# One step of a hybrid SSD and attention encoder: order of transposes, banks, evictions and operands at the edges of its stages

## The chip, the core and the metric

The kernel runs on one core of a Trainium2 chip. A core has TensorE (PE in the profile; PEld is its weight load), VectorE (DVE), ScalarE (ACT), GpSimd (POOL), SyncE (SP, which issues most DMAs here), an on-chip memory (SBUF) and eight accumulator banks (PSUM) of 512 float32 columns each. The metric is the device time of the whole program in microseconds, the median of several runs.

## The reference

One inference step over 1024 prompt tokens and 32 sample tokens with 1024 features, two layers, all float32:

```python
for i in range(DEPTH):                       # DEPTH = 2
    hn = rmsnorm(h, ln_w[i])
    if i == 0: y = ssd_mixer(hn, ...)        # in-projection, causal conv, chunked scan, gate, norm, out-projection
    else:      y = mla_mixer(hn, ...)        # low-rank q / kv, norms, rotary keys, block-causal attention, out-projection
    h = h + y
    g = sigmoid(rmsnorm(h, ple_norm_w[i]) @ ple_gate_w[i])
    h = h + (p[i] @ ple_up_w[i]) * g
```

Prompt and sample go through the same weights; the sample also has a convolution cache, a state and 1024 cached keys. The SSD mixer's projection gives, beside x, B, C and z, one step size dt for each of 32 heads: `dt = softplus(dt + bias)`, `Acs = cumsum(dt * A)` in chunks, and the scan weighs its rows with dt and with exponentials of differences of Acs.

## The kernel before

Activations lie with features on the 128 partitions and tokens on the free axis. A float32 product is made of three reduced ones: weights and operands are split into a high part (wh, hh, yh) and a rest (wl, hl, yl), and `gemm` (L239) issues, for every block k of 128 features, wh times high, wh times rest and wl times high into one bank. `load_weight` (L192) loads a block of 8 x 128 x 128 (SP), rounds it (ACT, L204) and takes the rest (POOL, L205); two or three such blocks have buffers at a time.

Nobody wrote down the order in which an engine's queue holds its work. A planner goes through the program with its own estimate of each instruction's duration and gives every engine a fixed order; buffers go to whoever's turn it is in that order, and an instruction waits for its operands and for the readers of the buffer that it takes over. So an edit at one place can move the order behind it.

**SSD phase** (`phase_ssd`, L301). The 1060 token columns (1024 prompt, a gap, 32 sample) go in three tiles of 384, 384 and 292. `normalise` (L318) makes the three tiles' normed operands hh and hl, 8 feature blocks each. `mblock` (L341) multiplies weight blocks with the tiles: a tile's result takes one of three mm banks and is evicted by `evac`. The heads are the first three blocks, dt (32 columns, `gemm_stacked`), B and C of group 0; L416 calls them tile by tile. Then follow, as `conv_block` (L487), blocks x(0,0) and x(0,1). Between them VectorE works out dt's 32 rows: `stk` holds dt, Acs and a third row set, and nine transposes (L482) bring it to `tokT`, tokens on the partitions. `stk` and its helpers lie in a pool that is closed after L483; the pool `work` (L485), with the scan's buffers ex, eb and y, is opened on the same space. For each of eight groups g the loop at L639 issues `scan_group(g)` (small products and exponentials in five chunks), the next group's B and C, the gate z of the group before, the next group's two x blocks, and `finish` of the group before. A block's raw result takes one of 6 `raw` buffers, a convolved one one of 6 `cx` buffers, and x, B and C hold theirs until their scan is done. In the last group `up_product` (L267) multiplies the layer's embeddings with their up weights in 8 blocks of three pieces of 352 columns, evicted by ACT (L290), and stores them.

**From there on** the columns are 1056 in two halves of 528 (HB), a half's product being two banks of 264 columns (`mm2`, three pairs). `gemm2` (L675) makes such a product: first all feature blocks for the left 264 columns, then all for the right. It is used by `phase_out` (L706; out-projections of both layers, with 16 and 8 feature blocks, output blocks m = 0..7, for each half), by `phase_ple` (L759; the gates) and by `phase_mla_in` (L797). `phase_out` loads a half's operands (yraw, five buffers), splits them on ACT and DVE into 33 buffers (yhl) that take both halves' rows in turn, and loads a weight block of 8 feature blocks wherever `part` (L727) comes to one. In the first half of the first out-projection three output blocks go ahead with the first 8 rows, while the others still come.

Then follow the MLA projections, the sample's attention, the prompt's attention, the second out-projection and the second gate; the change leaves the text of the attention parts as it was.

## Time and profile before

| | us |
|---|---|
| median of 3 runs (2000.93 to 2001.71) | 2001.32 |
| the profiled execution, its own time | 2003.33 |
| its span, first to last instruction | 2001.6 |
| PE busy (x12763) | 1927.1 |
| DVE busy | 1215.0 |
| ACT busy | 1069.0 |
| POOL busy | 999.9 |

In rows of the profile, `mm<-hh,wh` is a product that writes tile mm and reads hh and wh; L245 is its line in kernel.py, often a helper's. `128x292` are partitions and columns, x9 the number of instructions merged into one row. A row of the timeline has start, length, engine, line, operation, tiles; in brackets the idle time before it and what ended that. Products overlap their successors in PE's pipeline, so the step from start to start is what one costs, not its listed length. PEclk is the share of TensorE's clock that was granted.

### The profile page before, as it was taken

To read this page: it belongs to the slowest core of one execution; us is meant where nothing else is said; L and a number is where in the kernel's file an instruction comes from. 1 tells how busy PE (TensorE), PEld (TensorE's weight loads), DVE (VectorE), ACT (ScalarE), POOL (GpSimd) and SP (SyncE) were. 2 spreads that over 40 slices of the span, in tenths; PEclk is the share of its full clock that TensorE was granted. 3 is DMA by queue.
4 is the path that set the end of the run, shared out by engine and by line. 5 is a ranking of instruction groups with operands and counts; after the bars stand their busy time and mean duration, and the time that the engine had idled before them with its cause. 6 is when DMAs were issued, how large, how long until landed. Compare 5 with 4: busy or idle time off the path is not lost. (4 is left out here: it accounts for less than half of the span.)

```text
span 2001.6 us, 32532 instructions
## 1 busy us (share of the span) xinstructions
PE 1927.1 (96%) x12763; PEld 1773.0 (89%) x12763; DVE 1215.0 (61%) x1525; ACT 1069.0 (53%) x1998; POOL 999.9 (50%) x828
## 2 busy tenths in 40 slices
PE   7999999999999999999998999998899999999999
PEld 6989899999999998999998899777677877779999
DVE  7888674846657574452367543454667677755544
ACT  4345555454555558343244331777587878864331
POOL 5652424343443445554678452223556666645762
PEclk9999999999999999999999999999799999999999
DMA  4134433424233346553333221424412221416442
GB/s 141 43 83 104 93 86 83 106 74 103 75 94 91 78 118 233 173 174 123 101 120 121 83 75 65 152 85 124 102 47 57 61 72 41 119 57 196 125 129 72
DMA packets 110731, 204.26 MB, mean 102 GB/s; under 512 B 18225, under 2 KB 60721, under 8 KB 110449
## 3 DMA queue, kind: packets, MB, share of 16 engines
q1 hardware_dynamic: 105328, 193.04, 32.9%
q0 software_dynamic: 2944, 7.04, 1.8%
q8 instruction: 100, 1.64, 0.3%
q10 hardware_dynamic: 2304, 2.10, 0.3%
q14 instruction: 55, 0.44, 0.1%
HBM read 156.81 MB, written 38.83 MB: 98 GB/s over the span
## 5 line engine op out<-in xcount | busy, mean ns | idle before, releaser
L205 POOL TENSOR_TENSOR wl<-wraw,wh 128x1024 fp32r<-128x1024 f32 (+3 forms) x183 | 374.6, 2048 | 394.3 <-ACT wh L204 365.2
L245 PE MATMUL mm<-hh,wl 128*128 128x384 f32 (+1 forms) x1136 | 372.5, 328 | 0.0
L245 PE MATMUL mm<-hh,wh 128*128 128x384 f32 (+1 forms) x1136 | 372.3, 328 | 0.0
L245 PE MATMUL mm<-hl,wh 128*128 128x384 f32 (+1 forms) x1136 | 370.5, 326 | 0.0
L245 PE MATMUL pso<-yhl,wh 128*128 128x264 f32 x1536 | 283.8, 286 | 3.6 <-DVE yhl L259 2.2
L204 ACT ACTIVATE wh<-wraw 128x1024 fp32r<-128x1024 f32 (+3 forms) x181 | 157.2, 869 | 242.1 <-PE pso L245 103.7
L245 PEld LDWEIGHTS pso<-yhl,wh 128*128 128x128 f32 x1536 | 239.8, 189 | 5.3 <-DVE yhl L259 3.4
L245 PE MATMUL pso<-yhl,wl 128*128 128x264 f32 x768 | 219.2, 286 | 3.9 <-POOL wl L205 3.9
L245 PEld LDWEIGHTS mm<-hh,wh 128*128 128x128 f32 x1136 | 214.9, 189 | 3.5 <-issue 3.1
L245 PEld LDWEIGHTS mm<-hl,wh 128*128 128x128 f32 x1136 | 214.8, 189 | 1.2 <-issue 0.5
L245 PEld LDWEIGHTS mm<-hh,wl 128*128 128x128 f32 x1136 | 214.6, 189 | 0.8 <-issue 0.2
L496 DVE SCALAR_TENSOR_TENSOR cx<-raw,pv,cx 128x1060 f32<-128x1060 f32 x96 | 142.5, 1489 | 45.9 <-ACT cx L494 45.2
L559 ACT ACTIVATE ex<-ex,tokT 128x128 f32<-128x128 f32 (+1 forms) x288 | 87.0, 380 | 133.9 <-DMA ex<-acs_d 131.8
L245 PE MATMUL psi<-yhl,wh 128*128 128x264 f32 x832 | 153.6, 285 | 2.5 <-ACT yhl L258 1.7
L1346 PE MATMUL st<-qk 128*128 128x512 f32 (+2 forms) x576 | 150.3, 372 | 4.9 <-ACT pf L1352 4.1
L245 PEld LDWEIGHTS pso<-yhl,wl 128*128 128x128 f32 x768 | 145.2, 189 | 4.6 <-POOL wl L205 4.5
L245 PE MATMUL pg<-hH,wl 128*128 128x264 f32 x512 | 145.9, 285 | 2.5 <-POOL wl L205 2.5
L245 PE MATMUL pg<-hH,wh 128*128 128x264 f32 x512 | 145.9, 285 | 0.0
L245 PE MATMUL pg<-hL,wh 128*128 128x264 f32 x512 | 145.7, 285 | 0.0
L572 POOL TENSOR_TENSOR hm<-hT,cd_all 128x256 f32<-128x256 f32 x64 | 54.2, 848 | 160.4 <-DVE hT L574 95.4
L1328 DVE TENSOR_REDUCE mx<-s 128x1 f32<-128x128 f32 (+2 forms) x192 | 102.2, 550 | 52.0 <-PE s L1326 50.4
L245 PEld LDWEIGHTS psi<-yhl,wh 128*128 128x128 f32 x832 | 129.4, 188 | 3.9 <-ACT yhl L258 2.1
(546 smaller groups left out, 4649.5 us busy)
## 6 DMA issues: line engine op xcount, KB each, us to landing
wraw<-in_inW SPq DMA_DIRECT2D x48, 512.0 KB, 3.5
ex<-acs_d SPq DMA_DIRECT2D x32, 512.0 KB, 5.5
wraw<-in_outW SPq DMA_DIRECT2D x32, 512.0 KB, 3.7
yraw<-y_d SPq DMA_DIRECT2D x32, 264.0 KB, 4.6
u<-u_d SPq DMA_DIRECT2D x32, 264.0 KB, 2.9
eb<-ea_d SPq DMA_DIRECT2D x64, 128.0 KB, 4.0
y_d<-y SPq DMA_DIRECT2D x16, 512.0 KB, 2.8
wraw<-in_gateW SPq DMA_DIRECT2D x16, 512.0 KB, 3.5
```

The costliest lines, as they stand in the source:

```text
L204: nc.scalar.activation(wh, raw, AF.Copy)
L205: nc.gpsimd.tensor_tensor(wl, raw, wh.bitcast(F32), op=ALU.subtract)
L245: c.nc.tensor.matmul(ps, ww[:, k, :m], aa, start=first and k == 0 and i == 0, stop=last and k == n - 1 and i == 2)
L496: nc.vector.scalar_tensor_tensor(xh, raw[:, k : k + T1], pvc(c, "cw", 4 * b + k), xh, op0=ALU.mult, op1=ALU.add)
L559: nc.scalar.activation(e_, e_, AF.Relu, scale=-1.0, bias=tok(32)[:, i, h : h + 1])
L572: nc.gpsimd.tensor_tensor(hm.rearrange("p (h q) -> p h q", q=64), hT.rearrange("p (h q) -> p h q", q=64), bc_last(cd_all[:, hs, ch], 64), ...
L1328: nc.vector.tensor_reduce(mx[:, col : col + 1], ps[:, : (w if b else 128)], axis=AX.X, op=ALU.max)
L1346: nc.tensor.matmul(ps[:, :n], a_[:, ks], b_[:, q], start=t == 0, stop=t == 2)
```

## The change

Five things are edited:

- `up_product`: where four weight blocks are loaded at once (`nb > 1`, the SSD phase's call), the middle one of each three evictions is made by DVE instead of ACT.
- `mblock` takes `tags`, and the heads' second tile (j = 1) takes its three banks from the tags yd, yf and trb of the other PSUM pool, which the scan uses later, instead of mm.
- The nine transposes of `stk` get an order-only dependency on the last product of block x(1,1) (`c.product`, which `gemm` now returns): on PE they come behind it. No semaphore is added.
- `gemm2` goes over the feature blocks outside and over the two 264-column pieces inside: each feature block serves both pieces before the next one's turn. Its unused arguments are dropped.
- `phase_out`: for the second half the weights of m = 0, rows 0 to 7, are loaded ahead of the half's operands, not behind them; `part` skips the load that is already made.

```diff
@@ gemm
-            c.nc.tensor.matmul(ps, ww[:, k, :m], aa, start=first and k == 0 and i == 0, stop=last and k == n - 1 and i == 2)
+            p = c.nc.tensor.matmul(ps, ww[:, k, :m], aa, start=first and k == 0 and i == 0, stop=last and k == n - 1 and i == 2)
+    return p
@@ up_product
-            nc.scalar.activation(u[:, w_ * a : w_ * a + w_], ps[:, :w_], AF.Copy)
+            if nb > 1 and a % 2:
+                nc.vector.tensor_copy(u[:, w_ * a : w_ * a + w_], ps[:, :w_])
+            else:
+                nc.scalar.activation(u[:, w_ * a : w_ * a + w_], ps[:, :w_], AF.Copy)
@@ phase_ssd: mblock
-    def mblock(*blocks, ws=None, js=range(3), products=gemm):
+    def mblock(*blocks, ws=None, js=range(3), products=gemm, tags=None):
...
-            for w, (_, m, evac) in zip(ws, blocks):
-                ps = mm.tile([P, 512], F32, tag="mm", name="mm")
+            for i, (w, (_, m, evac)) in enumerate(zip(ws, blocks)):
+                ps = pc.tile([P, 512], F32, tag=tags[i], name="mm") if tags else mm.tile([P, 512], F32, tag="mm", name="mm")
...
-                    products(c, ps[:, :n], w, acts, slice(0, n))
+                    c.product = products(c, ps[:, :n], w, acts, slice(0, n))
@@ phase_ssd: heads
-        mblock(*heads, ws=early, js=(j,), products=gemm if j else gemm_rest_last)
+        mblock(*heads, ws=early, js=(j,), products=gemm if j else gemm_rest_last,
+               tags=("yd", "yf", "trb") if j == 1 else None)
@@ phase_ssd: transposes of stk
+        steps = []
...
-                nc.tensor.transpose(ps[:, i], stk[:, o : o + L], c.ident[:96, :96])
+                p = nc.tensor.transpose(ps[:, i], stk[:, o : o + L], c.ident[:96, :96])
+                steps.append(p.ins)
@@ phase_ssd: loop over groups
             x_block(g + 1, 1)
+            if g == 0:
+                for p in steps:
+                    tc.add_manual_dep(p, c.product.ins.name, mybir.DependencyInfo(
+                        mybir.DependencyClass.NoSync, mybir.DependencyReason.DATA), reason="late operand")
@@ gemm2
-def gemm2(c, ps, w, acts, kofs=0, nk=None, m=P, first=True, last=True):
-    for a in range(2):
-        gemm(c, ps[:m, a, :264], w, acts, slice(264 * a, 264 * a + 264), m, first, last)
+def gemm2(c, ps, w, acts, first=True, last=True):
+    n = len(acts)
+    for k in range(n):
+        for a in range(2):
+            gemm(c, ps[:, a, :264], [x[:, k : k + 1] for x in w], acts[k : k + 1], slice(264 * a, 264 * a + 264),
+                 first=first and k == 0, last=last and k == n - 1)
@@ phase_out
         acts = []
+        ws = {}
+        if hf:
+            ws[0] = load_weight(c, W[0][:, :8], 8, P)
...
-        ws = {}
-
...
-            if a == u:
+            if a == u and (a or m not in ws):
                 ws[m] = load_weight(c, W[m][:, u : u + 8], 8, P)
```

## The prediction

> **What bounds the kernel now.** I read the page first, then the waits of TensorE (PE), then busy times in stretches around each edge that the change touches, then single rows of the timeline there.

> ```profile
> span 2001.6 us, 32532 instructions
> PE 1927.1 (96%) x12763; PEld 1773.0 (89%) x12763; DVE 1215.0 (61%) x1525; ACT 1069.0 (53%) x1998; POOL 999.9 (50%) x828
> ```

> PE is busy 96% of the span, so the time is PE's work plus 74.5 us in which PE stands still, and the change leaves the number of products as it is. What can be won are single waits. The view of waits, PE's own, gives for each kind the sum, how often, and the longest:

> ```profile
> PE mm L230 <- ACT raw L360: 3.9, 1, 3.9
> PE pstk L482 <- issue: 3.9, 1, 3.9
> PE pso L245 <- POOL wl L205: 3.9, 3, 1.4
> PE mm L245 <- ACT upe L290: 3.0, 2, 1.5
> ...
> PE pso L245 <- DVE yhl L259: 2.2, 3, 1.1
> ...
> PE psi L245 <- ACT yhl L258: 1.7, 2, 1.3
> ```

> These six kinds, 18.6 us together, are what the edits aim at. A wait can cost more than its own length, as the granted clock in the stretches shows (columns: stretch, its length, then busy us and instructions of PE, weight loads, DVE, ACT, POOL, then PE's clock, DMA share, GB/s):

> ```profile
> 47.40:52.70 5.30, 5.30 (x22) 4.67 (x23) 0.40 (x1) 0.61 (x2) 0.80 (x1) 0.50 0.00 0
> 52.70:58.60 5.90, 5.90 (x45) 5.88 (x44) 0.81 (x2) 2.81 (x4) 3.22 (x2) 0.99 0.01 3
> 131.40:134.60 3.20, 3.20 (x16) 3.20 (x13) 3.20 (x7) 0.86 (x2) 0.14 (x2) 0.50 0.51 110
> 176.00:206.00 30.00, 27.84 (x186) 26.65 (x184) 28.25 (x27) 16.87 (x29) 9.57 (x6) 1.00 0.39 87
> 262.00:765.00 503.00, 502.32 (x3417) 480.56 (x3418) 320.44 (x402) 261.11 (x487) 207.77 (x215) 1.00 0.35 89
> 765.00:793.00 28.00, 23.90 (x143) 22.55 (x142) 13.47 (x11) 25.37 (x49) 14.90 (x10) 1.00 0.98 350
> 793.00:885.90 92.90, 92.80 (x766) 92.80 (x767) 41.06 (x31) 37.67 (x51) 49.09 (x22) 1.00 0.49 158
> 892.40:903.00 10.60, 7.31 (x31) 6.08 (x31) 8.34 (x6) 6.85 (x10) 5.49 (x3) 0.68 0.74 254
> 1086.00:1106.00 20.00, 15.88 (x112) 14.37 (x112) 12.59 (x12) 9.77 (x16) 13.18 (x9) 1.00 0.30 94
> ```

> After the first wait the clock stands at 0.50, and a 292-column product takes 5.30/22 = 0.24 us instead of 5.90/45 = 0.13. The same happens after the second (131.4 to 134.6), and around 892 to 903 (0.68).

> **The change part by part.**

> *Banks of their own for the heads' second tile (tags yd, yf, trb).* In the heads (tiles 0, 1, 2) the three products of tile 1 end together, and tile 2 needs a bank that tile 1 still holds. Rows of ACT and POOL there:

> ```profile
> 46.80 0.49 ACT L360 ACTIVATE raw<-mm 128x384 f32<-128x384 f32 x1
> ...
> 53.95 0.41 ACT L235 ACTIVATE xr<-mm 32x292 f32<-32x292 f32 x1 [5.94 <-PE mm L231]
> 54.26 2.08 ACT L204 ACTIVATE wh<-wraw 128x1024 fp32r<-128x1024 f32 x2
> ...
> 58.65 0.41 ACT L360 ACTIVATE raw<-mm 128x292 f32<-128x292 f32 x1 [1.86 <-PE mm L245]
> ```

> ```profile
> 47.71 0.80 POOL L339 TENSOR_TENSOR hl<-hf,hh 128x292 fp32r<-128x292 f32 x1 [0.45 <-ACT hh L338]
> 55.38 4.75 POOL L205 TENSOR_TENSOR wl<-wraw,wh 128x1024 fp32r<-128x1024 f32 x2 [6.87 <-PE mm L245]
> ```

> Tile 1 ends at 43.4 (row of 43.06 further down). Its evictions stand in ACT's queue behind the splits of tile 2, so the bank comes at 47.3, and tile 2, at half clock at first, ends at 58.6. With other banks tile 2 can start at 43.4. Its 64 products (8 rows of 2, 3 and 3) take 64 x 0.13 to 0.14 = 8.7 us, and the last operand is there at 48.5, before the last eighth needs it at 51: end at 52.1. Late next is the weight of the following block: its split (ACT) waits for dt's last product, then 0.31 + 1.04 on ACT, 0.08, and 2.37 on POOL, 3.8 in all. If the planner takes the operands in turns through the three heads, dt ends 0.8 before the others, and the weight is whole at 55.1; two products can go before. New start about 54.8 instead of 58.6: 3.8 us, of which I take 3.7. Bounds: 2 if this new wait brings the clock down once more; 6.5 if dt is put first and its weight slot is free early.

> *Transposes of stk behind block (1,1)'s last product.* Rows of PE, DVE, POOL and SP:

> ```profile
> 130.68 1.07 PE L482 MATMUL pstk<-cst,stk 96*128 96x96 f32 x9 [3.93 <-issue]
> 131.46 0.67 PE L245 MATMUL mm<-hh,wl 128*128 128x384 f32 x1
> 131.92 0.44 PE L245 MATMUL mm<-hh,wh 128*128 128x292 f32 x1
> ```

> ```profile
> 129.32 1.25 DVE L477 TENSOR_TENSOR stk<-w,stk 32x1060 f32<-32x1060 f32 x1
> ```

> ```profile
> 131.81 0.14 POOL L511 MEMSET y<- 128x8 f32 x2 [0.55 <-PE pstk L482]
> ```

> ```profile
> 131.78 0.38 SPq L525 DMA_DIRECT2D ex<-acs_d  x1
> ```

> The nine transposes stand in PE's queue from 126.7 and wait for stk, which DVE ends at 130.57. Behind them come one product of block (1,1)'s tile 1 (384 columns) and the 24 of its tile 2 (292), 25 x 0.14 = 3.5 us: with these ahead, PE reaches the transposes at 130.3 and waits 0.3. Raw gain 3.6, plus 1.5 from the half clock (3.20 us at 0.24 a product hold work of 3.20 x 0.13/0.24 = 1.7). But I don't count all of it. The transposes themselves don't move. The first scan's buffers lie where stk lay, so its ex load (131.78) and its y (131.81) start when they end: the scan stays where it is, while PE has used up 3.5 us of the work that filled its gaps. And from 176 to 206 the scan's end binds: DVE is busy 28.25 of 30 us with convolutions that need the buffers scan 0 frees. Products beyond those need raw buffers that these convolutions free. So I expect PE to stand still there instead, and count only the clock's 1.5. Bounds: 0 and 5.1.

> *Every third eviction of the up product on DVE.* From 765 to 793 ACT is busy 25.37 of 28 us, DVE 13.47. A row of ACT at the first of the two waits, which are 1.5 each, and DVE's nearest row for such a copy:

> ```profile
> 770.76 0.80 ACT L290 ACTIVATE upe<-mm 128x352 f32<-128x352 f32 x2
> ```

> ```profile
> 138.54 0.42 DVE L569 COPY hT<-st 128x256 f32<-128x256 f32 x1 [3.60 <-PE st L550]
> ```

> PE waits for a bank whose eviction stands behind a table load and the norm's two passes. Eight of 24 evictions go: ACT loses 8 x 0.4 = 3.2 us, DVE takes 8 x about 0.5 (352 columns, by the 256-wide copy's 0.42) = 4 us, in its idle half. With three banks, one in three freed early covers one product of about 1 us in each table load's shadow, so of 3.0 us I take 2.0 (0 if the planner hands the early bank out differently; 3.0 at best). If DVE were full there, the copies would sit on the path, 0.5 each.

> *Operands in turns for both halves (gemm2), weights ahead of operands.* The count of products and weight loads is the same. What moves is when an operand is last read: a block's row k is done after 6(k+1) products, not after 24 + 3(k+1). Rows around the edge between the first phase_out's halves:

> ```profile
> 877.91 2.25 ACT L258 ACTIVATE yhl<-yraw 128x528 fp32r<-128x528 f32 x4 [1.10 <-PE pso L245]
> ```

> ```profile
> 894.29 6.46 DVE L259 TENSOR_TENSOR yhl<-yraw,yhl 128x528 fp32r<-128x528 f32 x5
> ```

> ```profile
> 886.28 0.38 SPq L196 DMA_DIRECT2D wraw<-in_outW  x1
> ```

> ```profile
> 891.43 2.36 POOL L205 TENSOR_TENSOR wl<-wraw,wh 128x1024 fp32r<-128x1024 f32 x1 [7.40 <-ACT wh L204]
> ```

> A product takes 92.8/766 = 0.121 us. The second half's splits can't begin before the first half's last block lets go of a buffer (877.91, released by PE); in turns the first buffer comes free 21 x 0.121 = 2.5 us earlier, and the yraw loads behind it likewise. The weight load at 886.28 stood on SP behind six yraw loads that wait for DVE; 2.5 us earlier, its wl is whole at 891.3 instead of 893.8 and the wait of 1.4 goes. In the new order a row feeds 0.73 us of products instead of 0.36, so row 15 is wanted at 897 and comes at 900.75 - 2.5 = 898.2: about 1 us of waiting is left of the 10.60 - 7.31 = 3.3 there, and with it the clock stays up. In that stretch PE did 31 products; at 0.121 they need 3.8 us, with the waiting 4.8 of 10.6. Four of them are the norm's, which are slower, so I take a gain of 5.0 and not 5.8. Bounds: 1.4 (only the weight), 6.

> [...]

> The early load of the second half's first weight (one DMA on SP, a split on ACT and one on POOL, ahead of 16 operand loads and splits) I cost at nothing: its slots come free with the first half's last block either way, and its cover is that block's 48 remaining products, 5.8 us. Without that cover it would cost its chain, 3.8 as above.

> At the entry of the MLA projections (1086 to 1106, PE idle 4.1 us) turns remove most of psi's 1.7 us of waits for operands. Late next is the norm's sum on POOL:

> ```profile
> 1103.30 1.29 POOL L687 TENSOR_TENSOR acc<-acc,sq 128x528 f32<-128x528 f32 x1
> ```

> PE's norm product waits for it until 1104.6 whatever PE did before. I take 0.5; bounds -1.5 (the longer wait brings the clock down) and 2.5.

> *Sum*: 3.7 + 1.5 + 2.0 + 5.0 + 0.5 = 12.7 us. The profiled execution took 2003.3 us, 1.7 more than its span, and 2.0 over the median of the runs; against itself the sum gives 1990.6, against the median 2001.3 it gives **1988.6**.

> **The rivals.** *The transposes' gain is kept*: the planner finds other products or pulls the scan forward. Then +3.6: 1985.0. For it: in the window from 176 to 206 PE still has 27.84 of 30. Against: the row at 131.81.

> *The turns don't do what they should*: the edge at 892 is bound by the yraw loads, not by the slots. Then only the weight's 1.4 is left of 5.0, and with the heads at their lower 2: 1993.9. For it: those loads come one after another as DVE frees five buffers. Against: the split at 877.91 was released by PE.

> *Slower, by the planner.* All order is made by a planner from its own durations, and three edits move its start. From 262 to 765 the old order leaves PE 0.7 us of idle in 503; between 176 and 206 it leaves 2.2 in 30. If the new order puts scan steps of groups 1 to 7 as early as there, it costs 7 x 2.2 = 15 us and 7 half-clock stretches of 1.5, 26 in all: 2001.3 - 12.7 + 26 = 2014.6. It decides from four such groups (4 x 3.7 = 14.8 against 12.7). Against: those groups have had the same shape, and the edits only shift their beginning.

> *Slower, by changing banks.* gemm2 makes 5,088 products; in turns PE changes bank after every 3 instead of every 24 about 1,480 times more. If each change let the clock slip for one product, 0.24 instead of 0.13, it would cost 163 us: 2152. It decides from 9 ns a change. The heads' tile 1 already changes bank about three times in eight, and a plain product doesn't:

> ```profile
> 33.26 0.34 PE L245 MATMUL mm<-hh,wh 128*128 128x384 f32 x1
> ...
> 43.06 0.34 PE L245 MATMUL mm<-hh,wl 128*128 128x384 f32 x1
> ```

> ```profile
> 118.41 0.34 PE L245 MATMUL mm<-hh,wh 128*128 128x384 f32 x1
> ...
> 122.60 0.33 PE L245 MATMUL mm<-hh,wh 128*128 128x384 f32 x1
> ```

> That is 9.80 us for 56 steps, 0.1750, and 4.19 for 24, 0.1746: a change costs about 1 ns. [...]

> **How the numbers follow.** Forecast, gains of 9 to 16 us: 0.52. Transposes kept, 16 to 23: 0.16. Turns weak, 4 to 9: 0.17. Under 4 either way, several of the terms at their lower bounds: 0.09. Planner slower: 0.05; banks: 0.01. Best bounds together are 6.5 + 5.1 + 3.0 + 6 + 2.5 = 23, worst 2 + 0 + 0 + 1.4 - 1.5 = 1.9. The range from 1980 to 1998.5 leaves out the ends of both. What a measurement can tell from no change is 0.2%, 4.0 us: faster 0.85, same 0.09, slower 0.06.

> **What would show it.** Right: no wait of mm on raw near 43, and the following block's first products near 55; the transposes at the end of block (1,1) with a wait under 1 us, and more idle before 206; the ACT splits near 875 instead of 878, and a clock of 1.00 where 892 to 903 was; the product's step still 0.121. Wrong: a step over 0.125 in the phases with turns, idle over 5 us between 262 and 765, or a gain that comes from a stretch not named here.

## The result, and the profile after

The kernel after takes 1990.4 us (median of 6 runs, 1985.0 to 1993.2), the kernel before on the same chip 2001.5 (6 runs): ratio 0.994, 95% interval 0.9926 to 0.9954. The ratio is that of the means of the runs and stands for 12 us, between 9 and 15; the medians are 11.1 us apart. Measured once more on another chip (e12, below), the ratio is 0.994 again (0.9927 to 0.9954). The forecast was 1988.6, so the total is right. Not all of its terms are: those of the heads and the transposes were too small, that of the DVE evictions isn't found in its stage, that of the MLA entry had the wrong sign, and a cost that stood under the rivals, at another place, is what most of the runs below are about.

The page of the kernel after, its span and first row:

```profile
span 1989.1 us, 32537 instructions
PE 1922.0 (97%) x12763; PEld 1768.4 (89%) x12763; DVE 1217.8 (61%) x1533; ACT 1064.9 (54%) x1990; POOL 996.0 (50%) x828
```

The span is 12.5 us shorter: PE is busy 5.1 us less with the same 12763 products (the mean granted clock is 0.990 instead of 0.986) and idle 7.4 us less. TensorE's waits in the kernel after (sum, how often, longest):

```profile
PE pso L245 <- POOL wl L205: 3.6, 4, 1.3
...
PE n L710 <- POOL acc L703: 3.1, 2, 2.8
...
PE mm L245 <- ACT upe L294: 2.3, 2, 2.1
...
PE mm L245 <- DVE upe L292: 2.0, 2, 1.7
...
PE psi L245 <- ACT yhl L259: 1.2, 1, 1.2
PE psi L245 <- POOL wl L205: 1.1, 1, 1.1
...
PE pstk L488 <- PE mm L245: 0.6, 1, 0.6
```

The wait of mm on raw (3.9) is gone, and that of the transposes (3.9) is down to 0.6. The up product still waits 4.3 us, now on ACT and on DVE. At the MLA projections n waits for acc longer than before. The stretches that answer to those of the prediction (heads' tile 2, the block after it, the transposes, the end of scan 0, the long middle, the up product, the first phase_out's edge, the MLA entry in two parts):

```profile
42.50:52.10 9.60, 9.23 (x65) 8.25 (x64) 5.13 (x9) 5.80 (x12) 6.37 (x7) 1.00 0.01 2
52.10:58.00 5.90, 5.90 (x36) 5.90 (x35) 4.25 (x4) 3.96 (x6) 5.90 (x10) 1.00 0.61 178
123.30:128.00 4.70, 4.13 (x30) 4.15 (x30) 4.67 (x9) 2.29 (x5) 4.15 (x9) 1.00 0.58 168
169.00:199.00 30.00, 28.53 (x191) 27.35 (x190) 29.72 (x31) 17.78 (x30) 12.95 (x8) 1.00 0.30 75
249.50:753.00 503.50, 502.10 (x3413) 480.06 (x3412) 321.95 (x403) 261.71 (x488) 207.84 (x214) 1.00 0.36 90
753.40:781.70 28.30, 23.92 (x143) 22.51 (x142) 17.66 (x19) 21.40 (x39) 14.83 (x9) 1.00 0.97 347
880.00:890.60 10.60, 8.67 (x69) 8.25 (x69) 7.12 (x7) 6.20 (x10) 6.65 (x4) 1.00 0.90 314
1068.60:1091.40 22.80, 16.97 (x106) 15.28 (x106) 14.18 (x15) 11.32 (x18) 12.66 (x9) 0.87 0.29 94
1091.40:1096.00 4.60, 4.60 (x22) 4.50 (x21) 0.71 (x1) 1.99 (x3) 1.73 (x1) 0.51 0.40 114
```

Tile 2 runs at full clock from 42.5 and the next block begins at 52.1, without a wait. At the edge of phase_out PE does 69 products in 10.6 us instead of 31. The up product is as idle as before (4.4 us of 28.3). The MLA entry has become worse: 5.8 us of idle, and a clock of 0.51 behind it.

### The profile page after: what moved, and what is told of

The parts are those of the page before. It is cut to its first block, busy times and chain, and to the rows that moved or that the text cites. A ratio compares the mean times of both kernels' runs of the same rounds, so it can differ in the third digit from the quotient of the medians.

```text
span 1989.1 us, 32537 instructions
## 1 busy us (share of the span) xinstructions
PE 1922.0 (97%) x12763; PEld 1768.4 (89%) x12763; DVE 1217.8 (61%) x1533; ACT 1064.9 (54%) x1990; POOL 996.0 (50%) x828
## 5 line engine op out<-in xcount | busy, mean ns | idle before, releaser
L205 POOL TENSOR_TENSOR wl<-wraw,wh 128x1024 fp32r<-128x1024 f32 (+3 forms) x183 | 373.1, 2040 | 374.0 <-ACT wh L204 350.5
L245 PE MATMUL mm<-hh,wl 128*128 128x384 f32 (+1 forms) x1136 | 371.5, 327 | 0.0
L245 PE MATMUL mm<-hh,wh 128*128 128x384 f32 (+1 forms) x1136 | 371.1, 327 | 0.0
L245 PE MATMUL mm<-hl,wh 128*128 128x384 f32 (+1 forms) x1136 | 368.9, 325 | 0.0
L204 ACT ACTIVATE wh<-wraw 128x1024 fp32r<-128x1024 f32 (+3 forms) x181 | 157.1, 869 | 240.7 <-PE pso L245 96.5
L245 PE MATMUL pso<-yhl,wh 128*128 128x264 f32 x1536 | 282.9, 286 | 0.9 <-DVE hf L765 0.4
L245 PEld LDWEIGHTS pso<-yhl,wh 128*128 128x128 f32 x1536 | 238.9, 189 | 1.5 <-ACT yhl L259 1.0
L245 PE MATMUL pso<-yhl,wl 128*128 128x264 f32 x768 | 218.9, 285 | 3.6 <-POOL wl L205 3.6
L245 PEld LDWEIGHTS mm<-hh,wh 128*128 128x128 f32 x1136 | 213.5, 188 | 3.5 <-issue 3.2
L245 PEld LDWEIGHTS mm<-hl,wh 128*128 128x128 f32 x1136 | 213.8, 188 | 0.8 <-issue 0.2
L245 PEld LDWEIGHTS mm<-hh,wl 128*128 128x128 f32 x1136 | 213.5, 188 | 0.9 <-issue 0.2
L503 DVE SCALAR_TENSOR_TENSOR cx<-raw,pv,cx 128x1060 f32<-128x1060 f32 x96 | 144.7, 1511 | 44.0 <-ACT cx L501 43.4
L245 PE MATMUL psi<-yhl,wh 128*128 128x264 f32 x832 | 156.3, 289 | 1.6 <-ACT yhl L259 1.2
L245 PEld LDWEIGHTS pso<-yhl,wl 128*128 128x128 f32 x768 | 145.6, 190 | 4.6 <-POOL wl L205 4.6
L245 PE MATMUL pg<-hH,wl 128*128 128x264 f32 x512 | 145.5, 284 | 1.3 <-POOL wl L205 1.3
L245 PE MATMUL pg<-hH,wh 128*128 128x264 f32 x512 | 146.1, 285 | 0.0
L245 PE MATMUL pg<-hL,wh 128*128 128x264 f32 x512 | 145.7, 285 | 0.0
L579 POOL TENSOR_TENSOR hm<-hT,cd_all 128x256 f32<-128x256 f32 x64 | 53.6, 838 | 162.1 <-DVE hT L581 97.0
L245 PEld LDWEIGHTS psi<-yhl,wh 128*128 128x128 f32 x832 | 131.5, 192 | 2.9 <-ACT yhl L259 1.4
```

What stands on the lines that cost most here:

```text
L204: nc.scalar.activation(wh, raw, AF.Copy)
L205: nc.gpsimd.tensor_tensor(wl, raw, wh.bitcast(F32), op=ALU.subtract)
L245: p = c.nc.tensor.matmul(ps, ww[:, k, :m], aa, start=first and k == 0 and i == 0, stop=last and k == n - 1 and i == 2)
L503: nc.vector.scalar_tensor_tensor(xh, raw[:, k : k + T1], pvc(c, "cw", 4 * b + k), xh, op0=ALU.mult, op1=ALU.add)
L579: nc.gpsimd.tensor_tensor(hm.rearrange("p (h q) -> p h q", q=64), hT.rearrange("p (h q) -> p h q", q=64), bc_last(cd_all[:, hs, ch], 64), ...
```

## The experiments

**One part at a time (e1 to e4).** Each is the kernel before with one of the edits; the fifth edit (the second half's first weight ahead) goes with the turns in e4. In the built programs the order of all five engines' instructions is the same with that fifth edit and without it, so it moves nothing.

```diff
e1:  mblock(*heads, ws=early, js=(j,), products=gemm if j else gemm_rest_last,
+           tags=("yd", "yf", "trb") if j == 1 else None)
e2: +            for p in steps:
+                tc.add_manual_dep(p, c.product.ins.name, ...)
e3: +            if nb > 1 and a % 2:
+                nc.vector.tensor_copy(u[:, w_ * a : w_ * a + w_], ps[:, :w_])
e4: +    for k in range(n):
+        for a in range(2):
+            gemm(c, ps[:, a, :264], [x[:, k : k + 1] for x in w], acts[k : k + 1], ...)
```

> The kernel before with only the heads' banks changed (tags yd, yf, trb for tile 1). Theory (from the two traces): the dt head's 16 stacked products go first in tile 2, its weight slot comes free early, and no new wait appears: the 193rd product of mm begins 6.3 us earlier than before (52.1 against 58.45 us), and the whole time falls by as much, to about 1995. Rival 1 (the prediction's term): the following block waits for its weight, the 193rd product comes at 54.8, the time is 1997.6. Rival 2 (given back): the stage is 6.3 us shorter, but later stages, whose order is made anew, take it back, and the time is within 2 us of the kernel before.

> The kernel before with only the transposes of stk put behind block (1,1)'s last product. Theory (from the two traces): the gain is kept. The wait of 3.9 us ahead of the transposes falls under 1 us, no half clock follows, and the end of group 0's scan (the 37th product of st, 274.5 us in the kernel before) comes 5 to 6 us earlier, near 269; the time falls by about 6, to 1995. Rival (the prediction's term): scan 0 stays where it is, PE stands still before it instead, only the clock's 1.5 us are left: the 37th product of st at 273, the time 2000.

> The kernel before with only every third eviction of the up product moved to DVE. Theory: the waits of mm at the up product move from ACT to other evictions on ACT and to DVE's copies behind its splits of yhl, their sum stays about 4 us from the 3361st product of mm to the first pso (64.4 us in the kernel before, 64.9 in the one after): no change, 2001 to 2002. Rival (the prediction's term): 2 of the 3.0 us of waits go, that stretch takes 62.4 us, the time is 1999.3.

> The kernel before with only the turns of gemm2 and the second half's first weight ahead. Theory: from the 769th pso product to the first pg 5 us are gained (102.6 to 97.3), and the entry of the MLA projections gives nearly all back: from the first pg to the 97th psi product 118 us instead of 114.1, because the pg products now end earlier than the rows of DVE and ACT that they feed, and PE waits for the last rows and the norm's sum, with half clock after it. The time is 2000 to 2002. Rival: the loss at that entry belongs to the other edits' shift of the order; then it stays away here, that stretch takes 113 to 114 us, and the time is about 1996.

| | ratio to the kernel before | 95% interval |
|---|---|---|
| e1, heads' banks alone | 1.0035 | 1.0023 to 1.0047 |
| e2, transposes alone | 1.0039 | 1.0025 to 1.0053 |
| e3, DVE evictions alone | 1.0053 | 1.0036 to 1.0069 |
| e4, turns alone | 1.0036 | 1.0025 to 1.0046 |

Every single part makes the kernel slower, by 7 to 11 us, and all of them together make it 12 us faster. No theory had this: e1's second rival lets a later stage, ordered anew, take the gain back, but not more than that. In the stages that the edits touch the theories did better. e1's 193rd mm comes at 52.8 us and e2's 37th st at 267.7; e3's stretch takes 65.9 us, longer than before and longer than both its theory and its rival; e4 takes 97.0 us to the first pg and 116.2 behind it, between its theory's 118 and its rival's 113 to 114. So three of the four stages are 5.0 to 5.7 us shorter than in the kernel before, but in all four the prompt's attention, whose code no edit touches, took 10.6 to 12.8 us longer between the 25th product of s and the 2000th pso. There PE's order is one and the same in e1 to e4, and another one than before. The kernel after has the order of the kernel before from the 25th s on. Read from the built programs of all 16 combinations of the four edits, this stretch has three orders: the kernel before and the one with all four share one, eleven combinations have that of e1 to e4, three a third.

**The order alone (e5).** The kernel before, none of the edits; a list of positions and a chain of order-only dependencies put PE's 1692 products of the prompt's attention into the order of e1. On the other engines the planner follows by itself.

```diff
+ORDER = ((13, 2), (19, 2), (15, 4), (21, 28), (0, 2), ...)
...
+    row = [log[i] for a, n in ORDER for i in range(a, a + n)]
+    for p, q in zip(row, row[1:]):
+        tc.add_manual_dep(q, p.name, mybir.DependencyInfo(
+            mybir.DependencyClass.NoSync, mybir.DependencyReason.DATA), reason="order")
```

> The kernel before, with none of the five edits; only PE's order in the prompt's attention is replaced by the one that the planner gave to each of the four single edits (e1 to e4). Theory: that order alone costs 8 to 12 us, because with it PE waits more often for ACT and DVE there: from the 25th product of s to the 2000th pso 8 to 10 us more than before (404.6 us), all other stages as before, ratio 1.004 to 1.006. Rival: what e1 to e4 lost comes from gaps that their shift laid into other windows of the clock; then the order costs nothing and the ratio is within 0.001 of 1.

Ratio 1.0054 (1.0040 to 1.0067), 10.8 us; the stretch takes 416.4 us instead of 404.6. The theory holds, and the rival's 0.001 is outside the interval: this order by itself costs what the single edits lost in that stretch. TensorE's waits in the stretch, first in e5 (L1465 is the line that logs the products), then in the kernel before:

```profile
PE s L1465 <- DVE mx L1403: 5.5, 3, 2.0
PE o L1465 <- DVE pl L1442: 3.2, 6, 1.3
```

```profile
PE o L1370 <- DVE pl L1367: 0.9, 3, 0.6
...
PE s L1326 <- DVE mx L1328: 0.3, 1, 0.3
```

The waits on row maxima and on pl, both DVE's, grow from 1.2 to 8.7 us. One of them, on PE and then on DVE in e5:

```profile
1599.60 0.47 PE L1465 MATMUL s<-qk 128*128 128x448 f32 x1 [2.03 <-DVE mx L1403]
```

```profile
1595.03 1.77 DVE L1203 TENSOR_TENSOR rope<-rope,wsin 128x512 f32<-128x512 f32 x1
1596.73 0.68 DVE L1202 TENSOR_TENSOR rope<-rope,wcos 128x512 f32<-128x512 f32 x1
1597.33 1.75 DVE L1203 TENSOR_TENSOR rope<-rope,wsin 128x512 f32<-128x512 f32 x1
1599.00 0.55 DVE L1403 TENSOR_REDUCE mx<-s 128x1 f32<-128x384 f32 x1
```

The next s needs a bank; the row maximum that frees it stands in DVE's queue behind the rotary passes, so PE waits 2.0 us, and half clock follows from 1600.5 to 1603.9.

**The parts with the attention's order held (e6 to e9).** The same list, now with the order of the kernel before (e6, e7, e9) or after (e8).

> Only the heads' banks (as e1), with PE's order in the prompt's attention as in the kernel before. Theory: the 6 us of the heads now stay: ratio 0.997 (6 us). Rival 1 (the prediction's term): 3.7 us, 0.998. Rival 2: given back elsewhere, ratio 1.000 or more.

> Only the transposes behind block (1,1)'s last product (as e2), with PE's order in the prompt's attention as in the kernel before. Theory: scan 0 ends 5 us earlier and this is kept but for 1 to 2 us at the entry of the MLA projections: ratio 0.9975 to 0.9985 (3 to 5 us). Rival (the prediction's term): 1.5 us, ratio 0.9993.

> The kernel after without the DVE evictions of the up product, with PE's order in the prompt's attention as in the kernel after. Theory: those evictions are worth nothing by themselves (0 to 1 us against them), so the time is that of the kernel after, ratio to before 0.994, and the stretch from the 3361st mm to the first pso is 64.4 us instead of 64.9. Rival (the prediction's term): they are worth 2.0 us, ratio 0.995, the stretch is 66 to 67 us.

> Only the turns of gemm2 and the second half's first weight ahead (as e4), with PE's order in the prompt's attention as in the kernel before. Theory: 5 to 5.5 us are gained from the 769th pso product to the first pg, 0.8 lost in the 768 pso products before it, and 2 to 3 lost from the first pg to the 193rd psi product: 2 us in all, ratio 0.9985 to 0.9995. Rival (the prediction's terms): 5.0 and 0.5 are kept, ratio 0.997.

| | ratio to the kernel before | 95% interval |
|---|---|---|
| e6, heads' banks | 0.9983 | 0.9974 to 0.9992 |
| e7, transposes | 0.9980 | 0.9970 to 0.9989 |
| e8, all but the DVE evictions | 0.9953 | 0.9941 to 0.9966 |
| e9, turns and weight ahead | 0.9993 | 0.9983 to 1.0003 |

With the order held, heads and transposes gain, 3.4 and 4.0 us. The heads' value is nearer to the prediction's 3.7 than to the 6 of my later theory: alone they shorten their stage by 5.9, and the scan behind it gets 1.7 longer. e7 leaves out the prediction's 1.5 (0.9993). The turns gain 1.4 us, which the interval doesn't tell from nothing, and not 5.5: the rival falls. Without the DVE evictions the kernel after is at 0.9953; the intervals overlap, so by the times they are worth 0.0013, plus or minus 0.0018, or 2.6 us plus or minus 3.6. That leaves room for nothing as well as for the prediction's 2.0 (e8's rival had the ratio 0.995); but the rival's stretch of 66 to 67 us did not come (64.75 us without them, 64.88 with). The gains of e6, e7 and e9 add up to 8.8 us, and e8, which has these parts together, has 9.4.

**The order put on the kernel after (e11), and the kernel after again (e12).** e11 has all five edits and e1's order in the attention.

> The kernel after with all five edits; only PE's order in the prompt's attention is replaced by the one of e1 to e4. Theory: the order costs here what it costs alone (e5: 0.54%), so that all that the edits gained is used up: ratio to the kernel before 0.999 to 1.000. Rival: the edits and the order hang together, and with the edits it costs less than half as much: ratio 0.9965 or less.

> The kernel after as it is, once more, beside the three others on one chip. Theory: ratio 0.994, and in its trace other stretches of half clock than in the first one, since where a wait falls in the clock's windows differs from one execution to the next: the stretch from the first pg to the 193rd psi product (133.2 us in the first trace) differs by more than 1 us although the program is the same. Rival: that stretch is the program's doing, and comes out within 0.5 us of the first trace.

e11: ratio 0.9975 (0.9964 to 0.9986). Against 0.994 the order costs 0.0035, or 7 us; both numbers were missed, the theory's 0.999 by more than its half-width, the rival's bound 0.9965 by less. The stretch itself is 414.5 us against 407.0 and 403.3 in the two traces of the kernel after. That the order costs much with the edits too is shown; whether as much as without is not. e12: 0.994, and from the first pg to the 193rd psi 132.2 us instead of 133.2, with 3.4 us of half clock there instead of 10.2: a difference of just 1.0, so the length doesn't decide, but the half clock does.

**The wait at the MLA entry (e10).** POOL in the kernel after, at the new wait:

```profile
1086.67 1.90 POOL L198 TENSOR_TENSOR wraw<-wraw,pv 128x1024 f32<-128x1024 f32 x1 [5.93 <-DMA wraw<-in_miW]
1088.52 1.29 POOL L703 TENSOR_TENSOR acc<-acc,sq 128x528 f32<-128x528 f32 x1
```

PE has ended psi at 1087.04, and the last sum of squares stands behind a weight's scaling until 1089.8. In e10 DVE makes it:

```diff
-        nc.gpsimd.tensor_tensor(acc, acc, sq, op=ALU.add)
+        (eng or nc.gpsimd).tensor_tensor(acc, acc, sq, op=ALU.add)
...
+            sumsq(c, tmp, h1, accs[hf], m == 0, nc.vector if m == 7 and hf else None)
```

> The kernel after, in which the last row's square at the entry of the MLA projections is added to acc by DVE and not by POOL, where it stands behind a weight's scaling. Theory: the wait of n for acc (2.8 us at 1087) falls under 0.5, with it half a microsecond to 3.4 us of clock, and 2 to 5 us go: ratio to the kernel before 0.992 to 0.993. Rival: psi's next products then wait for the weight that POOL still has to make, and the time stays at 0.994.

Ratio to the kernel before 0.9910 (0.9895 to 0.9924): 1986.9 us where the kernel after, on the same chip, took 1991.9, and 6 us less by the ratios. It beats both kernels, by a little more than expected. DVE there:

```profile
1084.72 0.71 DVE L260 TENSOR_TENSOR yhl<-u,yhl 128x528 fp32r<-128x528 f32 x1 [0.71 <-ACT yhl L259]
1085.34 0.70 DVE L703 TENSOR_TENSOR acc<-acc,sq 128x528 f32<-128x528 f32 x1
```

```profile
1088.00:1095.00 7.00, 7.00 (x60) 7.00 (x59) 1.42 (x2) 2.80 (x5) 3.01 (x4) 1.00 0.24 75
```

The sum is there at 1086.0, PE doesn't wait, and the clock behind the entry is 1.00. From the first pg to the 193rd psi it takes 127.7 us, less than in any other trace (128.8 to 133.2). So the wait was the cost there, and DVE had room for the sum.

## Why the prediction was right, step by step

Thirteen traces (all but e10) have or lack each part, so each stage can be averaged over both kinds. Stretches run from the start of one product to that of another; in brackets lowest and highest. The stretch from the 193rd psi to the 25th s is left out: it takes 341.4 us with the turns and 341.3 without. The one from there to the 2000th pso is the planner's, below.

| stretch | part | without, us | with, us | difference | predicted |
|---|---|---|---|---|---|
| start to 193rd mm | heads' banks | 57.5 (56.6 to 58.4) | 52.8 (52.1 to 53.6) | -4.8 | -3.7 |
| to 37th st | transposes | 216.7 (216.1 to 217.7) | 211.0 (209.8 to 214.0) | -5.7 | -1.5 |
| to 3361st mm | transposes | 453.2 (452.6 to 454.2) | 455.0 (454.4 to 456.3) | +1.8 | 0 |
| to first pso | DVE evictions | 64.6 (64.4 to 64.9) | 64.9 (64.0 to 65.9) | +0.3 | -2.0 |
| to 769th pso | turns | 93.2 (93.1 to 93.8) | 93.9 (93.9 to 94.0) | +0.7 | 0 |
| to first pg | turns | 103.0 (101.3 to 105.0) | 97.4 (96.9 to 98.1) | -5.6 | -5.0 |
| to 193rd psi | turns | 130.0 (128.8 to 131.4) | 131.9 (130.5 to 133.2) | +2.0 | -0.5 |
| 2000th pso to end | turns | 137.5 | 137.1 | -0.4 | 0 |
| sum | | | | -11.7 | -12.7 |

The sum meets the 12 us measured because the errors cancel: 3.8 us too little for the heads (1.1), the transposes (2.4) and the turns in the out-projections (0.3), 4.8 too much for the evictions (2.3) and the MLA entry (2.5). That is luck, and so is it that the kernel with all edits kept the old order in the attention: with the order that eleven of the sixteen combinations have, its ratio is that of e11, 0.9975.

- *Heads*: right in kind, 1.1 short in its stage. The new wait for the next weight never came. The planner let dt's 16 products run ahead in tile 2 (the last begins at 47.94 us, 4 us ahead of the tile's end), so dt's weight slot came free early; that was the condition of the prediction's bound of 6.5. ACT and POOL in the kernel after:

```profile
48.59 1.99 ACT L204 ACTIVATE wh<-wraw 128x1024 fp32r<-128x1024 f32 x2
```

```profile
49.71 4.77 POOL L205 TENSOR_TENSOR wl<-wraw,wh 128x1024 fp32r<-128x1024 f32 x2 [1.92 <-ACT wh L204]
```

  The first of the two weights is whole near 52.1 (49.71 and half of 4.77), when PE wants it.
- *Transposes*: the failing step is "the scan stays where it is, while PE has used up 3.5 us of the work that filled its gaps". The transposes did stay (e7: 49.2 us after the 337th mm, as before), but PE did not stand still elsewhere in scan 0 instead: from the 193rd mm to the 37th st it is idle 6.2 to 7.8 us in the traces with this edit and 10.4 to 11.1 in those without. The scan's beginning came forward. DVE in e7:

```profile
131.35 1.17 DVE L486 COPY tokT<-pstk 128x384 f32<-128x384 f32 x3
...
136.53 0.42 DVE L572 COPY hT<-st 128x256 f32<-128x256 f32 x1 [1.00 <-PE st L553]
```

  From the first tokT to the first hT it is 5.2 us; before it was 6.3 (132.25 to 138.54), with DVE idle 3.60 for PE. The prediction had quoted that row, for its copy's length, and not read its bracket: scan 0 waited for PE, which still worked off the 25 products behind the transposes, at half clock (0.50 from 131.4 to 134.6). With these ahead, the scan's own products come earlier. DVE goes on being full (29.72 of 30 us in the stretch that had 28.25), and the idle time of PE that the prediction named as a sign stayed away (28.53 of 30 us busy where it was 27.84). So the rival that keeps the transposes' gain was right, with 3.9 us over both stretches where it would have had 5.1. Of the 5.7 us about 0.6 is order and not gain: four products of mm that stood ahead of the 37th st stand behind it with the edit. They are in the 1.8 us that come back in the groups behind; what the rest of that is stays open, since no single wait shows it.
- *DVE evictions*: not found in their stage. The failing step is "one in three freed early covers one product of about 1 us in each table load's shadow": of the two waits of 1.5 on ACT one fell to 0.3, the other grew to 2.1, and two on DVE came with them. ACT and DVE in the kernel after:

```profile
759.16 1.28 ACT L183 ACT_TABLE_LOAD   x1
760.46 1.09 ACT L183 ACTIVATE yr<-yr 128x1060 f32<-128x1060 f32 x1
761.45 0.63 ACT L259 ACTIVATE yhl<-yraw 128x528 fp32r<-128x528 f32 x1
761.98 0.80 ACT L294 ACTIVATE upe<-mm 128x352 f32<-128x352 f32 x2
```

```profile
768.33 3.50 DVE L260 TENSOR_TENSOR yhl<-yraw,yhl 128x528 fp32r<-128x528 f32 x2
771.75 0.51 DVE L292 COPY upe<-mm 128x352 f32<-128x352 f32 x1
```

  The table load still has two evictions behind it, and on DVE a copy of 0.51 stands behind splits of 1.75 each. The prediction took DVE for idle (13.47 of 28 us busy) and asked how full it was, not what stands ahead in its queue. But the waits on DVE are in this one trace. In e3, e11 and e12 there is none, ACT's are 0.3 and 2.1 again, PE's idle time in the stretch is 2.5 to 3.4 us instead of the 4.2 to 4.4 without the edit, and 3.4 or 6.8 us of half clock follow, which none of the traces without the edit has there. PE in the kernel after and in e12, and e12 behind the wait:

```profile
762.48 0.59 PE L245 MATMUL mm<-upx,wh 128*128 128x352 f32 x2 [2.06 <-ACT upe L294]
```

```profile
765.08 0.95 PE L245 MATMUL mm<-upx,wh 128*128 128x352 f32 x2 [2.06 <-ACT upe L294]
```

```profile
764.80:768.10 3.30, 3.02 (x10) 3.03 (x11) 3.30 (x4) 2.71 (x6) 1.41 (x1) 0.50 1.04 413
```

  So what the edit saves in waits for ACT, DVE's queue or the clock takes back.
- *Turns at the first phase_out*: right, 5.6 for 5.0. At an equal place in PE's work (the 433rd pso) the kernel after stands 11.0 us earlier; that is to be added to its times here. ACT, DVE, POOL and SP in the kernel after:

```profile
864.93 0.63 ACT L259 ACTIVATE yhl<-yraw 128x528 fp32r<-128x528 f32 x1
```

```profile
885.75 1.36 DVE L260 TENSOR_TENSOR yhl<-yraw,yhl 128x528 fp32r<-128x528 f32 x2
```

```profile
880.51 2.38 POOL L205 TENSOR_TENSOR wl<-wraw,wh 128x1024 fp32r<-128x1024 f32 x1 [4.90 <-ACT wh L204]
```

```profile
877.23 0.38 SPq L196 DMA_DIRECT2D wraw<-in_outW  x1
```

  The second half's splits begin at 864.9, which is 875.9 (875 was expected, 877.9 before), and the last row is there at 887.1, which is 898.1 (898.2 was expected, 900.75 before); the waits for operands are gone. One step failed: the weight. Its DMA still stands behind seven yraw loads, its wl is whole at 882.9, which is 893.9 as before (891.3 was expected), and of the wait of 1.4 for it about 1.2 are left; with a second, shorter one PE waits 1.9 us for weights at this edge, more than before. The fifth edit moved nothing, as said above. Not counted was 0.7 us more for the 768 products ahead, 1 ns each, which is as far as the changes of bank go: 9 ns a change, the break-even of the rival with the banks, would have been 2 us there and is not seen.
- *MLA entry*: the wrong sign. "Late next is the norm's sum on POOL" named the right wait and then left it at its old length. With psi done earlier it grew: its longest is 2.7 to 3.8 us in the six traces with the turns and at most 1.6 in the seven without, and e10 shows what it costs. From the first pg to the 193rd psi PE is idle 7.4 us on the mean with the turns and 6.6 without, and half clock lasts 6.2 us instead of 3.4. The two traces with the turns and neither the heads' nor the transposes' edit (e4, e9) have 130.6 us there, so most of the 2.0 us comes only with the other edits; why is open.
- *The planner*: the rival was there with 0.05, in scan groups 1 to 7, which kept their pace (idle over all of 249 to 753 is 1.4 us). It struck in the attention, at 11.3 us (404.8 without, 416.1 with that order), for every part alone. That it doesn't strike for the five together is what the prediction had no reason to expect. Which estimate tips the planner there is open.

## What to carry to other kernels

Where a planner makes the order, a part tried alone measures the planner's next choice as much as the part: hold the order of the stages that the edit doesn't touch, then compare. For a wait that an edit takes away, read the bracket of the consumer's row, who waits for whom, ahead of the share of busy time. And when something is evicted or added on another engine, look at the longest piece that can stand ahead of it in that queue, and not only at how busy the engine is. And see what the clock does behind a wait that has changed: at the up product two waits of 1.5 us became, in e12, one of 2.1 and one of 0.3, and 3.3 us at a clock of 0.50 followed.

## What the runs showed of the hardware

| trace | step, us | PE idle in it, us | clock in the next |
|---|---|---|---|
| before | 127.93 to 131.34 | 2.75 | 0.50 |
| before | 42.60 to 46.01 | 2.61 | 0.50 |
| after | 1734.18 to 1737.60 | 2.45 | 0.50 |
| before | 892.52 to 895.93 | 2.16 | 0.50 |
| after | 1085.65 to 1089.06 | 2.02 | 0.50 |
| after | 1075.41 to 1078.82 | 1.80 | 0.50 |
| before | 203.02 to 206.43 | 1.68 | 1.00 |
| before | 25.53 to 28.94 | 1.66 | 0.50 |
| before | 769.64 to 773.05 | 1.54 | 1.00 |
| after | 136.74 to 140.15 | 1.49 | 1.00 |
| before | 1438.65 to 1442.06 | 0.73 | 0.50 |

The five with over 2.0 us are all that the two traces have, and half clock follows each of them. Below that the idle time of a step doesn't tell: 1.66 us had half clock behind it, 1.68 had not, and 0.73 had. In the step from 892.52 the idle time belongs to two waits, 1.40 us until 893.85 and 1.06 until 896.16 (0.83 of it in the step), and not to a single long one.

Where half clock falls differs between executions of one program. The wait of 2.06 us at the up product, shown above, is in the kernel after and in e12, the same program: in the one the clock is 1.00 from 757.97 to 768.20 us, in the other 0.50 from 764.80 to 768.10. That it matters where in a step the wait lies is the author's reading, which no run tried by itself. What fits it: in the kernel after a step ends at 761.38, within the wait (760.42 to 762.48), and PE is idle 1.24 us in that step and 1.10 in the next; in e12 half clock begins at 764.7, 1.7 us into the wait.

The waits themselves differ too. The kernel before and e5 are the same program up to the attention; at the MLA entry psi waits for a row of yhl for 1.3 us at most in the one, and in e5 so:

```profile
PE psi L245 <- ACT yhl L258: 3.8, 1, 3.8
```

The clock stays at 1.00 in the one (its row from 1086 to 1106 stands in the prediction) and falls in the other:

```profile
1088.50:1095.30 6.80, 6.31 (x27) 6.01 (x28) 5.81 (x6) 5.77 (x9) 3.65 (x2) 0.50 0.27 91
```

This is also why a stage's length in one trace, 101.3 us without half clock (e3, e7) to 105.0 with 10.2 us of it (e1) for one and the same edge of phase_out, is no measure of an edit of 2 us: the table of stretches in the section on the prediction needs its six or seven traces a side.
